# The projection stage of a retention layer as a table of slots, with every engine's order stated

## The chip, the cores and the metric

The kernel runs on one core of one Trainium2 chip. The core has five engines with an instruction stream each: PE (matrix multiply), DVE (vector), ACT (scalar functions), POOL (GpSimd) and SP, which here only issues DMAs. The metric is the time of one execution on the device in microseconds (us); lower is better.

## The reference, cut to what matters

One inference step of a two-layer decoder: 1024 prompt tokens and 8 decode tokens of width 1024 go through a retention layer (called layer 1 here) and then a sliding-window attention layer. The change is in the first part of layer 1:

```python
h = rmsnorm(x, g_norm)
proj = h @ w_in                                  # 1024 -> 6144
q, k, v, gate = jnp.split(proj, [RET_QK, 2 * RET_QK, 2 * RET_QK + RET_V], axis=-1)
...
S_new = S * gamma_h + k_t^T v_t                  # for the 8 decode tokens: state_ret in, new state out
o_t = q_t S_new                                  # 4 heads, each state is 256 x 512 floats
```

All is float32. The kernel splits each operand into a high part of reduced precision and the rest, and multiplies three times (high by high, high by rest, rest by high).

## The kernel before, in words

**The stage.** `_trunk` runs the stages one after the other. The first one, everything from the pool `sa` up to `sa.close()`, computes the projection for all tokens, and beside it updates the retention state of the 8 decode tokens. Its results go to scratch memory in DRAM (`qks`, `vsc`, `gsc`, `vscr`), from where the next stage reads them. The columns of `w_in` are worked off in 20 sets: q, k and v for each of 4 heads, then 8 sets for the gate.

**Opening.** The tokens come in as 8 chunks of 128 and one of 8 decode rows (`xload`, on SP's queue). Each is normalised (`xnorm`: a square with sum on ACT, a scale on DVE, a power on POOL, the scaling on DVE), transposed on PE (`xtrans`), and its halves and their sums and differences are split into high part (`XH`, ACT) and rest (`XL`, DVE or POOL) by `xeven`, `xodd` and `xthird`. The first two sets (q and k of head 0) are multiplied in the ordinary way as soon as the first chunks are there: 16 calls of `plain`, 24 matmuls each (line 471).

**Main part.** The 18 other sets run through `run_set`, each as 7 products instead of 8 (a Strassen-Winograd scheme), every product for two groups of tokens. A product is 12 matmuls for q, k and gate (lines 362 to 364) and 24 for v (355 to 357). The weights' quarters, or their sums (lines 199 to 209, POOL), are split before use by `prep_unit` (line 210 on ACT, 211 on DVE or POOL). After each product `after` takes the result out of its bank (ACT at lines 398 and 404, DVE at 400, 402, 406, 408 and 410), and `spill` writes it out with a DMA on SP's queue. Weights are loaded by DMAs on ACT's queue (`raw_load`).

**Decode.** Each of 64 steps (4 heads, 2 halves of the columns, 8 tokens) loads 256 KB of state into `st` (line 258) and a broadcast row into `vb` (260), both on SP's queue. It scales the state by gamma on ACT (267), adds `kd * vb` on DVE in two pieces (269), forms `yd = q S` on ACT (271) and DVE (272), splits `yd` into `yh` (276, ACT) and `yl` (277, POOL), writes the state back (273, SP) and adds `yh` and `yl` to a result bank with two matmuls (286, 287). `st` has 3 buffers and `yd` one. The generator `decode` emits, per step, the load of one step, the matmuls of the step four earlier and the state update of the step two earlier; `work` advances it once per 5.3 us of estimated PE time.

**What sets the order.** PE's order is written out by hand: `manual_schedule` is in force for PE alone. For DVE, ACT, POOL and SP the framework's own scheduler orders the emitted instructions by priority and its estimate of when they are ready. On the chip each of these engines then runs its instructions strictly in that order, each waiting for the semaphores that its data and buffers need.

Of the kernel before, what the change touches and what calls it, by code (L numbers as in the profile page):

```python
# [75 lines left out]
def _trunk(ctx, tc, nc, a):  # L76
# [21 lines left out]

    def tr(out, in_, ident, start=True, stop=True):
        nc.tensor.matmul(out, in_, ident, is_transpose=True, start=start, stop=stop)  # L100
# [18 lines left out]
    B11, B21, B22, T4, T1, T2, T3 = range(7)  # L119
    B11, B21, T3, B22, T2, T1, T4 = range(7)  # L120
    sa = ExitStack()
    dcp = sa.enter_context(tc.tile_pool(name="dcp", bufs=1, reuse_waits="tile"))
# [12 lines left out]
    nc.vector.memset(xdecr.bitcast(F32), 0.0)  # L135
    nc.vector.memset(xdecd.bitcast(F32), 0.0)
    onehot = dcp.tile([128, 64], F32, name="onehot")
# [3 lines left out]
    XT = {}  # L141

# [5 lines left out]
    XH, XL = [[[None] * 7, [None] * 7] for _ in range(2)]  # L148
    xalloc(0, xp0, 0, 7)
    xalloc(1, xp1, 0, 3)  # L150
# [6 lines left out]
    def ring():  # L157
        return evp.tile([128, 516], F32, tag="ev", bufs=10, name="ev")
# [8 lines left out]
    def raw_load(s):  # L167
        s.raw = []
        if s.kind == "v":
            for sub in range(2):  # L170
                for j in range(2):
                    t = raw_tile().rearrange("p (k f) -> p k f", k=2)
                    nc.scalar.dma_start(out=t, in_=w_in_ret[512 * j + 256 * sub:512 * j + 256 * sub + 256, s.c0:s.c0 + 512]
                                      .rearrange("(k p) f -> p k f", p=128))
                    s.raw.append(t)
        else:
            for j in range(2):
                t = raw_tile().rearrange("p (k f) -> p k f", k=4)
                nc.scalar.dma_start(out=t, in_=w_in_ret[512 * j:512 * j + 512, s.c0:s.c0 + 256]
                                  .rearrange("(k p) f -> p k f", p=128))  # L180
                s.raw.append(t)
# [5 lines left out]
    ORDER = ("A11", "S2", "S1", "A12", "S3", "S4", "A22")  # L187

    def prep_unit(s, name, sub):
        kk = 512 // s.fw  # L190
        sh = [128, kk, s.fw]

        t_ = [("s1", 2), ("s2", 2)] if (s.kind, s.h, name) == ("k", 0, "A22") else [("wop", 14)] * 2
        hi, lo = [wq.tile(sh, F32R, tag=t, bufs=n, name=nm) for (t, n), nm in zip(t_, ("woh", "wol"))]
        if name[0] == "A":
            src = quad(s, int(name[1]) - 1, int(name[2]) - 1, sub)
        elif name == "S2":
            s1 = s.s1[sub] = wq.tile(sh, F32, tag="s1", bufs=2, name="s1")
            nc.gpsimd.tensor_tensor(s1, quad(s, 1, 0, sub), quad(s, 1, 1, sub), ALU.add)
            src = s.s2[sub] = wq.tile(sh, F32, tag="s2", bufs=2, name="s2")  # L200
            nc.gpsimd.tensor_tensor(src, s1, quad(s, 0, 0, sub), ALU.subtract)
        elif name == "S1":
            src = s.s1.pop(sub)
        elif name == "S3":
            src = wq.tile(sh, F32, tag="s1", bufs=2, name="s3")
            nc.gpsimd.tensor_tensor(src, quad(s, 0, 0, sub), quad(s, 1, 0, sub), ALU.subtract)
        else:
            src = s.s2.pop(sub)
            nc.gpsimd.tensor_tensor(src, quad(s, 0, 1, sub), src, ALU.subtract)
        nc.scalar.activation(hi, src, AF.Copy)  # L210
        (nc.gpsimd if name in ("A12", "A22") else nc.vector).tensor_tensor(lo, src, hi.bitcast(F32), ALU.subtract)  # L211
        s.op[name, sub] = (hi, lo)

    def mkset(kind, h, c0, kt=0):
        s = Set()
        s.kind, s.h, s.c0, s.kt = kind, h, c0, kt
        s.fw = 256 if kind == "v" else 128
        s.subs = 2 if kind == "v" else 1
        s.op, s.s1, s.s2 = {}, {}, {}
        return s  # L220
# [10 lines left out]
    units = [(s, name, sub) for i, s in enumerate(sets) for name in (ORDER if i >= PLAIN else  # L231
             ("A11", "A12", "A21", "A22")) for sub in range(s.subs)]
    nprep = [0]
    nraw = [0]
    AHEAD = 5

    def raw_to(n):
        while nraw[0] < min(n, len(sets)):
            raw_load(sets[nraw[0]])
            nraw[0] += 1  # L240

    def prep_to(n):

        while nprep[0] < min(n, len(units)):
            i = sets.index(units[nprep[0]][0])
            raw_to(i + (1 if i < PLAIN else 2))
            prep_unit(*units[nprep[0]])
            nprep[0] += 1

# [5 lines left out]
    def dec_load(h, hf, b):  # L255
        d = heads[h]
        st = dpo[0].tile([128, 2, 256], F32, name="st", bufs=3)
        nc.sync.dma_start(out=st, in_=state_ret[0, b, h, :, hf * 256:hf * 256 + 256].rearrange("(f p) e -> p f e", p=128))
        vb = dpo[0].tile([128, 256], F32, name="vb", bufs=3)
        nc.sync.dma_start(out=vb, in_=vscr[h, b, hf * 256:hf * 256 + 256].partition_broadcast(128))  # L260
        d["d", hf, b] = (vb, st)

    def dec_state(h, hf, b):
        d = heads[h]
        qd, kd16 = d["qd"], d["kd"]
        vb, st = d.pop(("d", hf, b))
        nc.scalar.activation(st, st, AF.Copy, scale=GAM[h])  # L267
        for f in range(2):
            nc.vector.scalar_tensor_tensor(st[:, f, :], vb, kd16[:, f, b:b + 1], st[:, f, :], ALU.mult, ALU.add)  # L269
        yd = dpo[0].tile([128, 256], F32, name="yd")  # L270
        nc.scalar.activation(yd, st[:, 0, :], AF.Copy, scale=qd[:, 0, b:b + 1])
        nc.vector.scalar_tensor_tensor(yd, st[:, 1, :], qd[:, 1, b:b + 1], yd, ALU.mult, ALU.add)  # L272
        nc.sync.dma_start(out=nrs[0, b, h, :, hf * 256:hf * 256 + 256].rearrange("(f p) e -> p f e", p=128), in_=st)
        yh = dpo[0].tile([128, 256], F32R, name="yh", bufs=2)
        yl = dpo[0].tile([128, 256], F32R, name="yl", bufs=2)
        nc.scalar.activation(yh, yd, AF.Copy)  # L276
        nc.gpsimd.tensor_tensor(yl, yd, yh.bitcast(F32), ALU.subtract)  # L277
        d["y", hf, b] = (yh, yl)

    def dec_mm(h, hf, b):  # L280
        d = heads[h]
        if hf == 0 and b == 0:
            d["od"] = odp.tile([128, 512], F32, name="od")
        od = d["od"][0:8, hf * 256:hf * 256 + 256]
        yh, yl = d.pop(("y", hf, b))
        mm(od, oneh_r[:, b, :], yh, start=(b == 0), stop=False)
        mm(od, oneh_r[:, b, :], yl, start=False, stop=(b == ND - 1))

    def dec_norm(h):
        d = heads[h]  # L290
        od = d["od"][0:8, :]
        on = ring()[0:8, 0:512]
        ss = dcp.tile([128, 1], F32, name="oss", bufs=2)
        rs = dcp.tile([128, 1], F32, name="ors", bufs=2)
        nc.scalar.activation(on, od, AF.Square, accum_out=ss[:8])
        nc.vector.tensor_scalar(ss[:8], ss[:8], 1.0 / DV, EPS, ALU.mult, ALU.add)
        rsq(rs[:8], ss[:8], 1)
        nc.vector.tensor_scalar(on, od, rs[:8], None, ALU.mult)
        d["ond"] = on

    def dec_out(h):
        on = heads[h].pop("ond")
        pt = odp.tile([128, 512], F32, name="od")
        for i in range(4):
            tr(pt[:, i * 8:i * 8 + 8], on[:, i * 128:i * 128 + 128], ident[:8, :8])
        nc.vector.tensor_copy(odT[:, 4 * h:4 * h + 4, :], pt[:, :32].rearrange("p (i t) -> p i t", i=4))

    dsteps = []
    for h_ in range(H):
        dsteps += [(h_, hf, b) for hf in range(2) for b in range(ND)] + [None]  # L310

    def decode():

        for i in range(len(dsteps) + 4):
            ld, mm_, st = [dsteps[j] if 0 <= j < len(dsteps) else None for j in (i, i - 4, i - 2)]
            if ld:
                dec_load(*ld)
            if mm_:
                dec_mm(*mm_)
                if mm_[1:] == (1, ND - 1):  # L320
                    dec_norm(mm_[0])
            elif i >= 4:
                dec_out(dsteps[i - 5][0])
            if st:
                dec_state(*st)
            yield

    pend = []
    spent = [0.0]

    def work(us):

        if pend:
            spent[0] += us
            if spent[0] > 5.3:
                spent[0] -= 5.3
                next(pend[0], None)


# [38 lines left out]
    def run_set(s):  # L378
# [7 lines left out]
        def out_of(key, t):  # L386
            if s.kind == "v":
                c[key, t] = ring()[:, 0:n]
            elif t == 0:
                r = ring().rearrange("p (t n) -> p t n", t=2)  # L390
                c[key, 0], c[key, 1] = r[:, 0], r[:, 1]
# [1236 lines left out]
```

## Time and profile before

| | us |
|---|---|
| runs of the kernel | 1477.28, 1478.95, 1483.41 (median 1478.95) |
| the profiled execution | 1477.93 |
| its span, first to last instruction | 1476.1 |
| its mean granted TensorE clock | 0.968 |

In the profile a group of instructions is named by line, engine and operation, then output<-input. "Busy" is the time in which an engine executes. PE's matmuls overlap each other, so that PE can be 100% busy at half its rate: the number of matmuls in a stretch (x) tells the rate. "Idle before" is time in which an engine stood still ahead of an instruction, with what released it. The clock is the share of its full clock that TensorE was granted.

### The profile page before, as it was taken

How to read it: one execution, taken by the hardware profiler on the slowest of the kernel's cores; microseconds unless marked ns; L12 is line 12 of the kernel's file. 1: busy time of each engine (PE TensorE's matmuls, PEld its weight loads, DVE VectorE, ACT ScalarE, POOL GpSimd, SP SyncE). 2: the span in 40 equal slices, each digit the busy share in tenths (PEclk: the TensorE clock that was granted, in tenths of full speed). 3: DMA queues.
4: the chain of work that ended last, by engine and by line, in shares of the span. 5: the costliest groups of instructions: out<-in, count | busy, mean ns of one | idle time of the engine just before them, and what ended most of it. 6: DMA issues, size and time to landing. Idle time of an engine off the chain costs nothing.

```text
span 1476.1 us, 26259 instructions
## 1 busy us (share of the span) xinstructions
PE 1357.8 (92%) x9545; PEld 1277.5 (87%) x9545; DVE 835.0 (57%) x1783; ACT 665.4 (45%) x1698; POOL 727.6 (49%) x825
## 2 busy tenths in 40 slices
PE   6899987988998898989997999999999999997998
PEld 5899987988998798967776788998899989996998
DVE  5735546546565455447676211223689888989511
ACT  5533423433435454446765011224567666666411
POOL 4654525534554454448887655546456555444100
PEclk9999998998999999989999999999999999999999
DMA  5325645645556555265653534453211110103433
GB/s 176 114 86 169 190 126 165 187 134 181 174 169 181 172 166 161 61 191 165 202 162 126 182 116 149 118 161 114 76 40 44 38 44 26 55 16 97 141 88 83
DMA packets 192376, 186.18 MB, mean 126 GB/s; under 512 B 12549, under 2 KB 172093, under 8 KB 192230
## 3 DMA queue, kind: packets, MB, share of 16 engines
q1 hardware_dynamic: 152288, 143.62, 32.6%
q10 hardware_dynamic: 39958, 40.88, 8.7%
q8 instruction: 75, 1.23, 0.4%
q14 instruction: 55, 0.45, 0.1%
HBM read 128.09 MB, written 57.41 MB: 126 GB/s over the span
## 4 chain that ended last, share of the span: by engine, by line
PE 38%; DVE 16%; issue 10%; DMA 10%; ACT 8%; POOL 7%; ACTq 0%; DVEq 0%; SPq 0%; POOLq 0%
DMA st<-in_state_ret_dram 6%; PE pj L928 4%; PE pj L926 4%; PE pj L927 4%; PE pj L877 3%; PE pj L879 3%; PE pj L878 3%; PE b L362 2%; PE b L363 2%; PE b L364 2%; PE tr L100 2%; ACT s L1286 1%; DVE yd L272 1%; DVE Sl L785 1%; POOL yl L277 1%
## 5 line engine op out<-in xcount | busy, mean ns | idle before, releaser
L362 PE MATMUL b<-xh,woh 128*128 128x258 f32 x784 | 231.4, 295 | 31.2 <-DVE ev L406 20.0
L364 PE MATMUL b<-xh,wol 128*128 128x258 f32 x784 | 228.4, 291 | 0.0
L363 PE MATMUL b<-xl,woh 128*128 128x258 f32 x784 | 228.1, 291 | 0.0
L362 PEld LDWEIGHTS b<-xh,woh 128*128 128x128 f32 x784 | 155.3, 198 | 37.2 <-DVE ev L406 22.2
L877 PE MATMUL pj<-A_hi,wh 128*128 128x384 f32 (+1 forms) x512 | 173.0, 338 | 0.6 <-ACT Qd L1185 0.6
L879 PE MATMUL pj<-A_hi,wl 128*128 128x384 f32 (+1 forms) x512 | 165.5, 323 | 0.0
L878 PE MATMUL pj<-A_lo,wh 128*128 128x384 f32 (+1 forms) x512 | 165.4, 323 | 0.0
L363 PEld LDWEIGHTS b<-xl,woh 128*128 128x128 f32 x784 | 155.9, 199 | 0.0
L364 PEld LDWEIGHTS b<-xh,wol 128*128 128x128 f32 x784 | 155.1, 198 | 0.0
L269 DVE SCALAR_TENSOR_TENSOR st<-vb,kd,st 128x256 f32<-128x256 f32 x128 | 85.0, 683 | 122.4 <-ACT st L267 119.1
L867 POOL TENSOR_TENSOR wl<-wr,wh 128x512 fp32r<-128x512 f32 (+1 forms) x68 | 124.3, 1846 | 52.5 <-DVE wh L866 20.5
L355 PE MATMUL b<-woh,xh 128*128 128x256 f32 x448 | 129.8, 290 | 10.0 <-DVE ev L406 10.0
L356 PE MATMUL b<-wol,xh 128*128 128x256 f32 x448 | 129.3, 289 | 0.0
L357 PE MATMUL b<-woh,xl 128*128 128x256 f32 x448 | 129.2, 288 | 0.0
L267 ACT ACTIVATE st<-st 128x512 f32<-128x512 f32 x64 | 40.2, 630 | 158.6 <-DMA st<-in_state_ret_dram 125.6
L277 POOL TENSOR_TENSOR yl<-yd,yh 128x256 fp32r<-128x256 f32 x64 | 56.0, 876 | 111.4 <-ACT yh L276 100.8
L1291 POOL TENSOR_TENSOR s<-s,sm 128x512 f32<-128x512 f32 x64 | 68.0, 1063 | 69.3 <-ACT ot L1326 14.3
L877 PEld LDWEIGHTS pj<-A_hi,wh 128*128 128x128 f32 x512 | 97.8, 191 | 1.1 <-ACT Qd L1185 0.9
L878 PEld LDWEIGHTS pj<-A_lo,wh 128*128 128x128 f32 x512 | 97.9, 191 | 0.0
L355 PEld LDWEIGHTS b<-woh,xh 128*128 128x128 f32 x448 | 87.9, 196 | 11.3 <-DVE ev L406 10.8
L879 PEld LDWEIGHTS pj<-A_hi,wl 128*128 128x128 f32 x512 | 97.4, 190 | 0.0
L211 POOL TENSOR_TENSOR wol<-raw,woh 128x512 fp32r<-128x512 f32 x48 | 64.2, 1337 | 56.9 <-ACT woh L210 52.4
(352 smaller groups left out, 3971.6 us busy)
## 6 DMA issues: line engine op xcount, KB each, us to landing
raw<-in_w_in_ret_dram ACTq DMA_DIRECT2D x48, 512.0 KB
st<-in_state_ret_dram SPq DMA_DIRECT2D x64, 256.0 KB
out_dram<-st SPq DMA_DIRECT2D x64, 256.0 KB
wr<-in_w_out_ret_dram SPq DMA_DIRECT2D x32, 512.0 KB
wr<-in_w_in_swa_dram SPq DMA_DIRECT2D x18, 512.0 KB
qks<-ev SPq DMA_DIRECT2D x64, 128.0 KB
vsc<-ev SPq DMA_DIRECT2D x32, 256.0 KB
vb<-vscr SPq DMA_DIRECT2D x64, 128.0 KB
```

Of the source, the lines that this page charges most:

```text
L269: nc.vector.scalar_tensor_tensor(st[:, f, :], vb, kd16[:, f, b:b + 1], st[:, f, :], ALU.mult, ALU.add)
L277: nc.gpsimd.tensor_tensor(yl, yd, yh.bitcast(F32), ALU.subtract)
L355: mm(dst, xh, wh, start=a and i == 0, stop=False, skip_group_check=True)
L356: mm(dst, xh, wl, start=False, stop=False, skip_group_check=True)
L357: mm(dst, xl, wh, start=False, stop=z, skip_group_check=True)
L362: mm(dst, wh, xh, start=a, stop=False, **sg)
L363: mm(dst, wh, xl, start=False, stop=False, **sg)
L364: mm(dst, wl, xh, start=False, stop=z, **sg)
L867: lo_eng[0].tensor_tensor(lo[:, js, :], raw[:, i:i + step, :], hi.bitcast(F32)[:, js, :], ALU.subtract)
L877: mm(ps, hi[:, k, fs], xh[:, k, t0:t1], start=first and k == ks[0], stop=False)
L878: mm(ps, hi[:, k, fs], xl[:, k, t0:t1], start=False, stop=False)
L879: mm(ps, lo[:, k, fs], xh[:, k, t0:t1], start=False, stop=last and k == ks[-1])
```

## The change

The mathematics, the sets, the products and PE's matmuls per product stay. What changes:

- **All engines in a stated order.** Within the pool `sa` the manual schedule also holds for ACT, DVE, POOL and SP.
- **A table of slots.** Each `plain` and each product for one token group is a slot with an estimated PE time; the running sum of these is a clock. The evacuation of slot n is emitted in slot n+1, its spill in slot n+2 (n+3 where a SiLU comes between). Everything else has a planned time on that clock: a product's high split 6.5 us ahead of its first use (7.8 and 6.3 us for the two parts of v), the rest 1.4 us after it, weight loads up to 13 us ahead of their first use, and the decode steps every 5.3 us.
- **Decode rearranged.** The load of a step is planned 10.5 us ahead of its first arithmetic. ACT forms `kv = kd * vb` in two pieces (new tile, one buffer), and one DVE instruction over 128x512 does `st = gamma * st + kv`; the scale of the state on ACT is gone. `yd` comes 13.9 and 15.3 us after the load, `yh` 16.8, `yl` 18.2, the matmuls are placed at the first slot boundary after 20.4 us. `st` gets 4 buffers instead of 3, `yd` 2 instead of 1, `yl` 1 instead of 2.
- **Opening rearranged.** The gain row is broadcast by one DMA instead of two matmuls with a row of ones. The raw weights of the first two sets are loaded on SP's queue between the chunks. The chunks are normalised in place; the transposed copies of the even chunks are taken by DVE (ACT before); the scale ahead of the power is on POOL (DVE before). The 16 plain slots each carry a written list of chunk work, and transposes of chunks 1, 3, 4, 6, 5, 7 open the slots 2, 3, 6, 7, 9, 10. The decode rows' columns are split piece by piece on DVE.
- **Buffers.** The ring of 10 evacuation buffers becomes four rings (3, 2, 2, 2); split weights have 12 buffers instead of 14; `qd`/`kd` 4 instead of 2.

```diff
+    sa.enter_context(tc.manual_schedule(engines={ET.Activation, ET.DVE, ET.Pool, ET.SP}))
...
-    def dec_load(h, hf, b):
-        d = heads[h]
-        st = dpo[0].tile([128, 2, 256], F32, name="st", bufs=3)
+    def dec_load(d, h, hf, b):
+        d["st"] = dt("st", 4, (128, 2, 256))
+        nc.sync.dma_start(out=d["st"], in_=sview(state_ret, h, hf, b))
+        d["vb"] = dt("vb", 3)
+        nc.sync.dma_start(out=d["vb"], in_=vscr[h, b, hf * 256:hf * 256 + 256].partition_broadcast(128))
...
-        nc.scalar.activation(st, st, AF.Copy, scale=GAM[h])
-        for f in range(2):
-            nc.vector.scalar_tensor_tensor(st[:, f, :], vb, kd16[:, f, b:b + 1], st[:, f, :], ALU.mult, ALU.add)
+    def dec_kv(d, h, hf, b):
+        d["kv"] = dt("kv", 1, (128, 2, 256))
+        for f in range(2):
+            act(d["kv"][:, f, :], d["vb"], AF.Copy, scale=heads[h]["kd"][:, f, b:b + 1])
+
+    def dec_st(d, h, hf, b):
+        dve.scalar_tensor_tensor(d["st"], d["st"], GAM[h], d["kv"], MUL, ADD)
+
+    def dec_y0(d, h, hf, b):
+        d["yd"] = dt("yd", 2)
+        act(d["yd"], d["st"][:, 0, :], AF.Copy, scale=heads[h]["qd"][:, 0, b:b + 1])
+        nc.sync.dma_start(out=sview(nrs, h, hf, b), in_=d["st"])
...
+    def slot(us, pe, *ops):
+        s = Slot()
+        s.t, s.pe, s.ops = clock[0], pe, ops
+        clock[0] += us
+        slots.append(s)
+        return len(slots) - 1
+
+    def later(n, fn, *a):
+
+        at.setdefault(n, []).append((fn, a))
+
+    def when(t, fn, *a):
+        ev.append((t, len(ev), fn, a))
...
+        us = 2.84 if s.kind == "v" else 1.43
+        slot((us + (0.95 if dec else 0.0)) * (1.045 if s is not sets[2] else 1.0), pe)
+        later(n + 1, evac, s, j, t)
...
+    STEP, GAP = 5.3, 6.5
+    pes = []
+    t0 = 0.0
+    for h in range(H):
+        t0 = max(t0 + GAP, sets[3 * h + 2].end + 10.0)
+        for hf in range(2):
+            for b in range(ND):
+                d = {}
+                for dt_, fn in ((0.0, dec_load), (10.5, dec_kv), (12.3, dec_st), (13.9, dec_y0), (15.3, dec_y1),
+                                (16.8, dec_yh), (18.2, dec_yl)):
+                    when(t0 + dt_, fn, d, h, hf, b)
+                pes.append((t0 + 20.4, dec_mm, (d, h, hf, b)))
+                m = t0 + 20.4
+                t0 += STEP
...
+    nc.scalar.dma_start(out=gb, in_=norm_ret[0].partition_broadcast(128))
+    nc.scalar.dma_start(out=ident, in_=a["c1"][:, 0:128])
+    act(warm, warm, AF.Silu)
+    for c in (8, 0, 2):
+        xload(c)
+    for r in range(2):
+        raw_load(q0, r, nc.sync)
+    for c in (1, 3):
+        xload(c)
+    for r in range(2):
+        raw_load(k0, r, nc.sync)
+    for c in (4, 6, 7):
+        xload(c)
...
+    for n, s in enumerate(slots):
+        while pes and pes[0][0] <= s.t:
+            _, fn, args = pes.pop(0)
+            fn(*args)
+        s.pe()
+        for fn, args in at.pop(n, ()):
+            fn(*args)
+        for fn, args in s.ops:
+            fn(*args)
+        end = s.t if n + 1 == len(slots) else slots[n + 1].t
+        while ev and ev[0][0] < end:
+            _, _, fn, args = ev.pop(0)
+            fn(*args)
```

More of the change, by code (lines that the diff above doesn't have):

```diff
@@ L688, in _trunk @@
+    rest = sorted([(t, 0, fn, args) for t, _, fn, args in ev] + [(t, 1, fn, args) for t, fn, args in pes],
+                  key=lambda e: e[:2])
+    for _, _, fn, args in rest:
+        fn(*args)
+    print("stage", clock[0], "decode", t0)
     sa.close()
```

751 lines of the change are left out of this document (376 added, 375 removed).

## The prediction

> **What bounds the kernel now.** I read the page first, then the busy time by stretches, then who waits for whom in the projection stage, then the chain that ended last inside one slow stretch.
>
> ```profile
> span 1476.1 us, 26259 instructions
> ...
> PE 1357.8 (92%) x9545; PEld 1277.5 (87%) x9545; DVE 835.0 (57%) x1783; ACT 665.4 (45%) x1698; POOL 727.6 (49%) x825
> ```
>
> PE looks full, but overlapping matmuls count as busy, so the rate has to be read from the counts. The next rows are stretches: length, PE, PEld, DVE, ACT and POOL busy (with counts), granted clock, DMA share, GB/s. The last one was asked for PE alone.
>
> ```profile
> 87.00:638.00 551.00, 502.08 (x3952) 490.55 (x3950) 297.05 (x495) 221.47 (x474) 257.77 (x310) 0.95 0.52 156
> 280.00:320.00 40.00, 40.00 (x340) 39.60 (x339) 18.73 (x28) 14.31 (x29) 16.18 (x19) 1.00 0.47 140
> 200.00:240.00 40.00, 31.05 (x210) 29.37 (x209) 18.57 (x26) 12.45 (x26) 13.86 (x12) 0.84 0.52 161
> 420.00:440.00 20.00, 20.00 (x171) 19.76 (x170) 13.04 (x19) 9.06 (x18) 10.67 (x10) 1.00 0.79 243
> 520.00:540.00 20.00, 20.00 (x165) 19.77 (x165) 13.78 (x23) 10.77 (x25) 11.06 (x15) 0.98 0.58 171
> ...
> 140.00:160.00 20.00, 17.56 (x144) 1.00 0.69 191
> ```
>
> From 280 to 320 us PE runs 340 matmuls in 40 us, 0.1176 us each at a clock of 1.00: the full rate. The main part of the stage, 87 to 638 us, holds 3952 of them. At the full rate that is 464.9 us; it takes 551. So 86.1 us are lost there, and that is what this stage could give back. The stretch from 200 to 240 shows how: 210 matmuls need 24.7 us, PE is idle 8.95, and the other 6.35 go to a clock of 0.84.
>
> The waits in the stage (in total, times, longest):
>
> ```profile
> ACT st L267 <- DMA st<-in_state_ret_dram: 125.6, 39, 6.4
> DVE st L269 <- ACT st L267: 119.1, 42, 6.4
> ...
> PE b L362 <- DVE ev L406: 20.0, 8, 4.2
> PE b L362 <- DVE ev L410: 10.7, 8, 2.4
> PE b L355 <- DVE ev L406: 10.0, 4, 3.7
> ```
>
> ACT stands before the state's scale until the state has landed, DVE stands before line 269 for ACT, and PE waits for banks that DVE has not emptied. The chain inside the slow stretch (start, length) says why the load comes late:
>
> ```profile
> 212.77 6.83 DMA st<-in_state_ret_dram
> ...
> 219.71 0.64 ACT st L267
> ...
> 220.77 0.68 DVE ev L406
> ...
> 222.83 1.51 DVE yd L272
> ...
> 224.36 2.70 DMA st<-in_state_ret_dram
> ```
>
> A load starts when a `yd` ends, since its buffer comes free then; it takes 2.7 to 6.8 us; the next `yd` on ACT is queued behind the scale that waits for this load. With 3 buffers, only one load is in flight at a time: 11.6 us from one load to the next here, where PE's order wants a step each 5.3 us.
>
> **The change part by part: the main part.** The decode chain's order is undone at its root. The load is now planned 12.3 us ahead of the one instruction that needs it, against 6.8 us for the longest load above, with four buffers instead of three. The wait does not vanish, it moves: DVE now waits for the state itself. Queued behind it are DVE's evacuations and weight splits, and PE waits for those. A lead of 12.3 against 6.8 is the cover; without it each microsecond of lateness would stop DVE. ACT's new wait is for `vb`, 10.5 us after its issue. SP's load waits for the write-back of the step four earlier, issued 7.3 us before it; the spills stand behind that.
>
> Durations for the parts (busy, mean ns):
>
> ```profile
> L269 DVE SCALAR_TENSOR_TENSOR st<-vb,kd,st 128x256 f32<-128x256 f32 x128 | 85.0, 683 | 122.4 <-ACT st L267 119.1 <-ACT woh L210 1.7 <-DMA vb<-vscr 1.2
> L211 DVE TENSOR_TENSOR wol<-s,woh 128x512 fp32r<-128x512 f32 x88 | 74.3, 846 | 27.4 <-ACT woh L210 23.8 <-PE b L471 2.7 <-issue 0.2
> L211 POOL TENSOR_TENSOR wol<-raw,woh 128x512 fp32r<-128x512 f32 x48 | 64.2, 1337 | 56.9 <-ACT woh L210 52.4 <-PE b L364 2.4 <-PE b L357 1.9
> L277 POOL TENSOR_TENSOR yl<-yd,yh 128x256 fp32r<-128x256 f32 x64 | 56.0, 876 | 111.4 <-ACT yh L276 100.8 <-DVE st L269 5.4 <-PE b L357 4.7
> L267 ACT ACTIVATE st<-st 128x512 f32<-128x512 f32 x64 | 40.2, 630 | 158.6 <-DMA st<-in_state_ret_dram 125.6 <-issue 18.9 <-DVE ev L408 6.1
> L271 ACT ACTIVATE yd<-st,qd 128x256 f32<-128x256 f32 x64 | 32.6, 509 | 64.4 <-POOL yl L277 62.7 <-DVE st L269 1.6
> L533 DVE TENSOR_TENSOR xl<-b,xh 128x512 fp32r<-128x512 f32 x16 | 10.4, 685 | 7.2 <-ACT xh L532 7.2
> L513 DVE SCALAR_TENSOR_TENSOR raw<-xq,rs,gb 128x1024 f32<-128x1024 f32 x7 | 10.0, 1428 | 6.7 <-POOL rs L114 6.7
> L533 DVE TENSOR_TENSOR xl<-ev,xh 128x512 fp32r<-128x512 f32 x8 | 9.5, 1203 | 0.0
> L511 DVE TENSOR_SCALAR ss<-ss 128x1 f32<-128x1 f32 x8 | 1.0, 145 | 2.1 <-ACT raw L510 2.1
> ```
>
> Decode work: ACT loses 64 scales (40.2 us) and gains 128 pieces of 128x256, nearest line 271, so 128 x 0.509 = 65.2: plus 25. DVE loses 128 pieces (85.0) and gains 64 of 128x512; on the line between 0.683 for 256 columns and 1.428 for 1024 that is 0.93 each, 60 us: minus 25 (bounds: 54 us by line 211's 0.846, 87 by twice 0.683). None of it is on the path as long as the engines keep up: squeezed into some 480 us, DVE would be busy (297.05 - 25)/480 = 57%, ACT (221.47 + 25)/480 = 51%, POOL 257.77/480 = 54%. From 520 to 540 us they were at 69, 54 and 55% while PE ran 165 matmuls of 170 possible. The DMAs, 551 x 156 = 86 MB, would need 179 GB/s; from 420 to 440 us they ran at 243 with PE at its full 171.
>
> What is late next is the end of the decode chain. `yl` is planned at 18.2 and takes 0.876, so it ends at 19.1, and the matmuls stand at 20.4: a margin of 1.3 us. In front of the chain can lie one weight split on DVE (0.846) and one on POOL (1.337), 2.2 us together. The worst is then 0.9 us of PE waiting in each of 64 steps, 58 us; the best is nothing. The matmuls are put at the first slot boundary after their time, which with slots of 12 x 0.1176 = 1.41 us adds 0.7 on average. I take 0.2 us per step, nearer to the lower end: 13 us. A bank has at least three slots, 4.2 us, between its evacuation's start and PE's next use, as much as the longest wait that the table of waits shows, and those came from the 6.4 us holds that go. So the evacuations get no price. Main part: 86.1 - 13 = **73 us gained** (bounds 28 and 86).
>
> Does a short wait cost more than itself? From 140 to 160 us PE was idle 2.44 us in pieces and the clock stayed at 1.00; from 200 to 240, with longer ones, each idle microsecond cost 15.3/8.95 = 1.7. I price short waits at themselves. The Trainium skill, "TensorE: Matmul & The Clock Gate", section "A second HAM failure mode: psum-queue depth-cycling", speaks against that: frequent tiny idles between groups of matmuls can be enough to make the clock swing. By that rule the 13 us would cost 13 x 1.7 = 22 and the sum would be 9 us higher; the row from 140 to 160 us does not bear it out.
>
> **The opening.**
>
> ```profile
> 9.92 1.28 DVE L513 SCALAR_TENSOR_TENSOR raw<-xq,rs,gb 128x1024 f32<-128x1024 f32 x1 [0.67 <-POOL rs L114]
> ...
> 13.63 1.28 DVE L513 SCALAR_TENSOR_TENSOR raw<-xq,rs,gb 128x1024 f32<-128x1024 f32 x1
> ```
> ```profile
> 14.97 1.97 PE L100 MATMUL b<-ident,raw 128*128 128x128 f32 x8 [1.74 <-DVE raw L513]
> 19.30 2.09 PE L471 MATMUL b<-xh,woh 128*128 128x258 f32 x8 [2.36 <-ACT xh L532]
> 21.19 1.77 PE L471 MATMUL b<-xh,wol 128*128 128x258 f32 x8
> 22.80 1.12 PE L471 MATMUL b<-xl,woh 128*128 128x258 f32 x8
> ...
> 84.93 0.28 PE L355 MATMUL b<-woh,xh 128*128 128x256 f32 x1
> ```
> ```profile
> 16.15 0.63 ACT L210 ACTIVATE woh<-raw 128x512 fp32r<-128x512 f32 x1 [2.68 <-DMA raw<-in_w_in_ret_dram]
> ```
> ```profile
> 5.00:10.00 5.00, 2.24 (x9) 1.00 1.04 401
> ```
>
> The first projection matmul is at 19.30 us. Chunk 2 was scaled at 13.63, behind a weight split that waited; in the stated order it follows chunk 0, at 9.92 + 1.28 + 0.2 = 11.4. Its transposes then end at 11.4 + 1.3 + 2.0 = 14.7, and a high split of 0.6 lets PE start at 15.3. The raw weights, which landed at 16.15, come ahead of chunks 1 to 6 in SP's queue. The broadcast of the gain moves another 0.5 MB while the DMAs are full (share 1.04, 401 GB/s): 1.3 us, which can eat some of it. **4 us gained** (bounds 0 and 6).
>
> From 19.30 to 84.93, 65.6 us, run 16 x 24 matmuls and 6 x 8 transposes: 432 x 0.1176 = 50.8 us. The first 16 took 3.5 us (19.30 to 22.80) instead of 1.9, a start that stays: 52.4. What is left, 13.2 us, was waiting. In the slots 5 to 11 of the list DVE gets 16 operations from a bank (0.685), 7 from SBUF (1.203), 2 scalings (1.428) and 18 small ones (0.145): 11.0 + 8.4 + 2.9 + 2.6 = 24.9 us, against 7 x 24 + 4 x 8 = 200 matmuls, 23.5 us. DVE is thus a little short there. I leave 4 us of waiting: **9 us gained** (bounds 0 and 13).
>
> The other edits have one answer, nothing: fewer ring and weight buffers are reused more than a set later or 11 us after their product, and the copies that go from ACT to DVE are counted in the slots above.
>
> **The sum.** 4 + 9 + 73 = 86 us off the profiled execution's 1477.93: 1391.9. That execution took 1.8 us beyond its span, and is 1.0 under the median of the runs, 1478.95; so **1393 us** for a median.
>
> **The rivals.** *The decode chain becomes PE's wait at its worst.* Every step is 0.9 us late, 58 us instead of 13: 1393 + 45 = 1438. For it: margins of 1.3 us behind queues whose single operations take as long. Against it: the slot boundaries, and that a PE that waits hands all others time.
>
> *The hold moves to DVE and grows (slower).* SP's load waits for a write-back, the DMAs carry 15% more per microsecond, and a late state now stops the engine that empties the banks. It ends slower when the stage's waits exceed 86.1 + 13.2 + 7.4 = 107 us, 1.7 us in each step; as DVE has 12.3 us of lead, loads would have to take some 14 us on average. At 2 us a step, 128 instead of 13, it gives 1393 + 115 = 1508. Against it: the longest load seen is 6.8 us.
>
> *The clock swings on short waits*, the skill's rule above: 1402.
>
> *The change does not do what it says*: some resource that I do not see paces the decode steps as before, the 73 us stay, and only the opening gains or loses: about 1477, no change. The stretches with PE at full rate inside the decode stage speak against it.
>
> **How the numbers follow.** My case has 0.68, the clock rival 0.05, the late chain 0.18: all faster, 0.91. No change has 0.03, the hold on DVE 0.06. The lower end takes all bounds at their best, 6 + 13 + 86 = 105 off: 1374. The upper end is the late chain, 1438. About 0.5%, 7.4 us, is what a measurement can tell from no change.
>
> **What would show it.** Right: the first projection matmul near 15 us, the first v matmul near 72, the last gate evacuation near 552; ACT's wait for the state gone, and DVE's wait for it under some 10 us in total; state loads at an even 5.3 us; long stretches at 170 matmuls per 20 us with the clock at 1.00; PE's remaining waits mostly on `yl`. Wrong: DVE idle on the state load or SP on the write-back for microseconds at a time, a clock under 0.95 in the stage, or PE waiting for weight splits. The stages behind should keep their length; if they don't, the sum is wrong in a term that I left out.

## The result, and the profile after

| | before | after |
|---|---|---|
| median (range, runs), us | 1479.56 (1477.28 to 1483.41, 4) | 1387.83 (1386.91 to 1390.77, 4) |
| profiled execution, us | 1477.93 | 1390.77 |
| its span, us | 1476.1 | 1389.0 |

The ratio of after to before is 0.938, with a 95% interval of 0.936 to 0.941: 91.7 us less in the medians, 87.1 us less between the two profiled spans. The profiled execution of after is the slowest of its four runs, 2.9 us above the median.

The page of the kernel after begins so, and its chain that ended last is made up so (shares by engine):

```profile
span 1389.0 us, 26326 instructions
...
PE 1320.1 (95%) x9541; PEld 1249.1 (90%) x9541; DVE 804.3 (58%) x1737; ACT 679.3 (49%) x1754; POOL 739.5 (53%) x830
...
PE 65%; DVE 15%; ACT 6%; issue 6%; POOL 4%; DMA 3%; ACTq 0%; DVEq 0%; POOLq 0%; SPq 0%
```

The same line of the page of before:

```profile
PE 38%; DVE 16%; issue 10%; DMA 10%; ACT 8%; POOL 7%; ACTq 0%; DVEq 0%; SPq 0%; POOLq 0%
```

PE's share of the chain went from 38 to 65%, and the DMAs' from 10 to 3%. The boundaries of the stage in the timeline of after (start, length): first projection matmul, first v matmul, last evacuation of a gate product.

```profile
14.09 0.74 PE L555 MATMUL b<-xh,woh 128*128 128x258 f32 x4
...
70.82 0.28 PE L332 MATMUL b<-woh,xh 128*128 128x256 f32 x1
...
546.54 0.43 DVE L380 TENSOR_TENSOR evp<-b,evp 128x258 f32<-128x258 f32 x1 [0.97 <-PE b L341]
```

In before, the first two stand in the prediction (19.30 and 84.93), and the third is:

```profile
638.18 0.43 DVE L410 TENSOR_TENSOR ev<-b,ev 128x258 f32<-128x258 f32 x1 [0.97 <-PE b L364]
```

So the 87.1 us are 5.2 ahead of the first projection matmul, 8.9 in the opening (65.6 to 56.7), 77.5 in the main part (553.2 to 475.7), and -4.5 in the stages behind (837.9 to 842.5).

Busy time by stretches in after (length, PE, PEld, DVE, ACT, POOL, clock, DMA share, GB/s; the last was asked for PE alone):

```profile
71.00:546.00 475.00, 473.77 (x3966) 468.92 (x3966) 261.79 (x438) 240.02 (x542) 267.66 (x312) 1.00 0.60 182
220.00:240.00 20.00, 20.00 (x168) 19.66 (x167) 10.32 (x22) 10.35 (x24) 13.06 (x16) 1.00 0.82 258
...
80.00:540.00 460.00, 460.00 (x3853) 1.00 0.62 187
```

The whole main part comes close to the density that before had in its good stretches, 3966 matmuls in 475 us for 340 in 40, and the clock stays at 1.00. What PE waited for in the stage, the five longest (in total, times, longest):

```profile
PE tr L840 <- DMA qk<-qks: 7.3, 2, 5.4
PE pd L105 <- DMA ident<-const_c_dram: 7.2, 1, 7.2
PE b L105 <- DVE xq L441: 2.3, 2, 2.1
PE b L555 <- POOL wol L223: 1.5, 1, 1.5
PE b L333 <- DVE wol L223: 1.2, 1, 1.2
```

The first belongs to the next stage, the next three to the start and the opening. Of the main part only the last row is left, 1.2 us: PE waits neither for a bank nor for `yl`. The waits of the others that touch the decode step:

```profile
ACT yd L269 <- DVE st L265: 42.6, 25, 3.1
POOL yl L281 <- PE od L288: 41.6, 18, 5.1
...
DVE st L265 <- ACT kv L262: 7.2, 8, 1.5
```

The two waits of over 100 us each for the state (ACT's for the load, DVE's for ACT) are gone, and no such wait of DVE for the load stands in their place. The waits left are long only in sum, and POOL's is for PE: the chain runs ahead of PE and not behind it.

### The profile page after: what moved, and what is told of

Read it like the earlier page. It is cut to its first block, busy times and chain, and to the rows that moved or that the text cites. A ratio compares the mean times of both kernels' runs of the same rounds, so it can differ in the third digit from the quotient of the medians.

```text
span 1389.0 us, 26326 instructions
## 1 busy us (share of the span) xinstructions
PE 1320.1 (95%) x9541; PEld 1249.1 (90%) x9541; DVE 804.3 (58%) x1737; ACT 679.3 (49%) x1754; POOL 739.5 (53%) x830
## 4 chain that ended last, share of the span: by engine, by line
PE 65%; DVE 15%; ACT 6%; issue 6%; POOL 4%; DMA 3%; ACTq 0%; DVEq 0%; POOLq 0%; SPq 0%
PE b L339 7%; PE b L341 7%; PE b L340 7%; PE b L333 4%; PE b L334 4%; PE b L332 4%; PE pj L1037 4%; PE pj L1035 4%; PE pj L1036 4%; PE pj L986 3%; PE pj L987 3%; PE pj L988 3%; ACT s L1395 2%; PE tr L105 2%; DVE Sl L894 1%
## 5 line engine op out<-in xcount | busy, mean ns | idle before, releaser
L339 PE MATMUL b<-xh,woh 128*128 128x258 f32 x784 | 222.1, 283 | 0.0
L341 PE MATMUL b<-xh,wol 128*128 128x258 f32 x784 | 221.7, 283 | 0.0
L340 PE MATMUL b<-xl,woh 128*128 128x258 f32 x784 | 221.3, 282 | 0.0
L339 PEld LDWEIGHTS b<-xh,woh 128*128 128x128 f32 x784 | 148.1, 189 | 1.2
L340 PEld LDWEIGHTS b<-xl,woh 128*128 128x128 f32 x784 | 148.6, 190 | 0.0
L341 PEld LDWEIGHTS b<-xh,wol 128*128 128x128 f32 x784 | 148.0, 189 | 0.0
L332 PE MATMUL b<-woh,xh 128*128 128x256 f32 x448 | 125.7, 281 | 0.0
L223 POOL TENSOR_TENSOR wol<-raw,woh 128x512 fp32r<-128x512 f32 x52 | 68.8, 1330 | 47.9 <-ACT woh L218 47.0
L333 PEld LDWEIGHTS b<-wol,xh 128*128 128x128 f32 x448 | 84.3, 188 | 1.4 <-DVE wol L223 1.4
L1395 ACT ACTIVATE s<-s,mx 128x256 f32<-128x256 f32 x128 | 64.0, 502 | 43.9 <-DVE mx L1392 39.6
```

The lines of the kernel that those rows point to most:

```text
L223: eng.tensor_tensor(lo, src_of(s, name, sub), hi.bitcast(F32), SUB)
L332: mm(dst, xh, wh, start=a and i == 0, stop=False, skip_group_check=True)
L333: mm(dst, xh, wl, start=False, stop=False, skip_group_check=True)
L339: mm(dst, wh, xh, start=a, stop=False, **sg)
L340: mm(dst, wh, xl, start=False, stop=False, **sg)
L341: mm(dst, wl, xh, start=False, stop=z, **sg)
```

## The experiments

In all of them the whole reference is computed. Two numbers come back throughout. The **main part** is the time from the first v matmul to the last gate evacuation, as above (before 553.2 us, after 475.7). The **lead** is the time from the issue of a state's load on SP to the start of the first instruction that uses the state (ACT's scale in before, DVE's line 265 in after); given is the median over the 64 steps: before 3.7 us, after 14.1. One pair of each, first the load's issue and then the use, in after:

```profile
215.44 0.46 SPq L255 DMA_DIRECT2D st<-in_state_ret_dram  x1
...
228.74 0.70 DVE L265 SCALAR_TENSOR_TENSOR st<-st,kv 128x512 f32<-128x512 f32 x1
```

and in before:

```profile
231.82 0.37 SPq L258 DMA_DIRECT2D st<-in_state_ret_dram  x1
...
234.75 0.63 ACT L267 ACTIVATE st<-st 128x512 f32<-128x512 f32 x1 [4.79 <-DMA st<-in_state_ret_dram]
```

13.3 us against 2.9, the latter with ACT standing still for 4.79 us ahead of the use.

My theory at first was that the buffers and the arithmetic, which take the load out of ACT's way, carry most of the gain, with the order only keeping the loads ahead. (The prediction itself counted on the lead, and didn't say which part of the change makes it.) The rival was that the stated order carries it. The first four kernels tell them apart.

**The framework's order for all engines but PE**, all else as after:

```diff
-    sa.enter_context(tc.manual_schedule(engines={ET.Activation, ET.DVE, ET.Pool, ET.SP}))
```

> The changed kernel without the one line that puts ACT, DVE, POOL and SP under the stated order; the program, its buffers and its decode arithmetic stay. My theory (the loop in the decode chain cost the time; fewer dependences and more buffers open it, the stated order keeps the loads ahead): 1410 us, DVE's wait for the state between 20 and 80 us in the stage. Rival 'order alone': 1450 to 1478. Rival 'decode data flow alone': 1386 to 1395, no wait of PE in the main part.

Measured: 1463.17 us (1459.33 to 1465.52), ratio to before 0.987 [0.985, 0.989]. Main part 545.0, lead 4.1. Waits and a stretch of it:

```profile
DVE st L264 <- DMA st<-in_state_ret_dram: 103.6, 39, 6.4
ACT kv L261 <- DVE st L264: 89.0, 36, 6.7
...
PE od L287 <- POOL yl L280: 34.0, 10, 7.5
...
PE b L338 <- DVE evw L375: 9.0, 4, 4.9
```
```profile
80.00:540.00 460.00, 411.11 (x3278) 0.95 0.59 173
```

This kernel has the four buffers, the new arithmetic and the table's order of emission, and yet the wait is back on another engine: DVE now stands before the state for 103.6 us, and ACT behind DVE, since `kv` has one buffer. How this reaches PE can be followed in the timeline:

```profile
172.53 0.69 DVE L264 SCALAR_TENSOR_TENSOR st<-st,kv 128x512 f32<-128x512 f32 x1 [4.86 <-DMA st<-in_state_ret_dram]
173.25 0.51 ACT L261 ACTIVATE kv<-vb,kd 128x256 f32<-128x256 f32 x1 [3.39 <-DVE st L264]
...
174.84 1.27 POOL L222 TENSOR_TENSOR wol<-raw,woh 128x512 fp32r<-128x512 f32 x1 [6.03 <-ACT woh L217]
...
176.06 0.72 POOL L280 TENSOR_TENSOR yl<-yd,yh 128x256 fp32r<-128x256 f32 x1
...
176.84 0.38 PE L287 MATMUL od<-yl,oneh_r 128*8 128x256 f32 x1 [5.06 <-POOL yl L280]
```

DVE stands for the load, ACT's next `kv` for DVE, the high split behind it in ACT's queue comes late, POOL stands for that split, `yl` is next in POOL's queue, and PE waits 5.06 us for `yl`. So most of PE's waits come through `yl` (34.0 us) and fewer through the evacuations, though the load is at the root. Nearly all of the main part's gain went with the stated order, 69.3 of 77.5 us, and 3.9 of the opening's 8.9. The theory falls.

**Before with after's decode buffers only:**

```diff
-        st = dpo[0].tile([128, 2, 256], F32, name="st", bufs=3)
+        st = dpo[0].tile([128, 2, 256], F32, name="st", bufs=4)
...
-        yd = dpo[0].tile([128, 256], F32, name="yd")
+        yd = dpo[0].tile([128, 256], F32, name="yd", bufs=2)
...
-        yl = dpo[0].tile([128, 256], F32R, name="yl", bufs=2)
+        yl = dpo[0].tile([128, 256], F32R, name="yl")
```

(The ring of evacuation buffers has 9 instead of 10, to make room.)

> The kernel before with 4 state buffers instead of 3 and 2 of yd instead of 1 (paid for by one yl buffer and one evacuation buffer less), nothing else. My theory: two loads can be in flight, ACT's wait for the state falls from 125.6 us to about 60 and the time to about 1435. Rival 'order alone': 1470 to 1480. Rival 'decode data flow alone': about 1470, since the scale on ACT still waits for the load.

Measured: 1470.46 us (1470.34 to 1471.44), ratio 0.992 [0.991, 0.994]. Main part 545.9, lead 4.3. ACT's wait has not become shorter but longer than the 125.6 us of before:

```profile
ACT st L267 <- DMA st<-in_state_ret_dram: 155.0, 45, 6.9
...
SPq L258 <- DVE yd L272: 56.6, 25, 7.6
```

The second row is SP's: the load still waits there for a `yd` to end and free a buffer. The timelines show where the fourth buffer went. In before, 62 of the 64 loads are issued with two earlier steps still short of their `yd`; here 61 are issued with three. But in 55 of 64 steps (52 in before) the scales of all earlier steps have begun by then. So the order uses the new buffer to scale one more state ahead of its `yd`, and the load is not issued earlier relative to its own use. What the buffers alone are worth isn't quite shown, since they are paid for: with one `yl` PE's waits for it rise from 0.8 to 20.2 us.

**Before with after's arithmetic** (`st` keeps 3 buffers; `yd` 2, `yl` 1, the ring 9):

```diff
-        nc.scalar.activation(st, st, AF.Copy, scale=GAM[h])
+        kv = dpo[0].tile([128, 2, 256], F32, name="kv")
         for f in range(2):
-            nc.vector.scalar_tensor_tensor(st[:, f, :], vb, kd16[:, f, b:b + 1], st[:, f, :], ALU.mult, ALU.add)
+            nc.scalar.activation(kv[:, f, :], vb, AF.Copy, scale=kd16[:, f, b:b + 1])
+        nc.vector.scalar_tensor_tensor(st, st, GAM[h], kv, ALU.mult, ALU.add)
```

> The kernel before with the new decode arithmetic (kv on ACT, one DVE instruction on the state) and 2 yd buffers (one yl and one evacuation buffer less), 3 state buffers, order by the framework. My theory: ACT no longer stands behind a load, yd comes earlier, 1425. Rival 'order alone': 1470 to 1480. Rival 'decode data flow alone': 1400 to 1410 (all but the opening).

Measured: 1494.98 us (1494.12 to 1495.56), ratio 1.009 [1.007, 1.010]: slower than before. Main part 568.5, lead 3.8.

```profile
DVE st L270 <- DMA st<-in_state_ret_dram: 118.7, 42, 6.6
...
PE od L288 <- POOL yl L278: 44.6, 14, 6.2
```

The hold did move to DVE, as the prediction's slower rival had it, and the main part is 15.3 us longer. PE's longest waits are for `yl`, along the same path as in the framework's order above: a held DVE stops ACT's `kv` too, and POOL's splits behind that. Whether a second `kv` buffer or a second `yl` would avoid it was not tried.

**After with the old arithmetic**, in the stated order:

```diff
-        d["kv"] = dt("kv", 1, (128, 2, 256))
-        for f in range(2):
-            act(d["kv"][:, f, :], d["vb"], AF.Copy, scale=heads[h]["kd"][:, f, b:b + 1])
+        act(d["st"], d["st"], AF.Copy, scale=GAM[h])
...
-        dve.scalar_tensor_tensor(d["st"], d["st"], GAM[h], d["kv"], MUL, ADD)
+        for f in range(2):
+            dve.scalar_tensor_tensor(d["st"][:, f, :], d["vb"], heads[h]["kd"][:, f, b:b + 1], d["st"][:, f, :], MUL, ADD)
```

> The changed kernel with the old decode arithmetic in the new places: at 10.5 us ACT scales the state, at 12.3 us DVE adds kd*vb in two pieces. My theory and 'order alone': the load has 10.5 us of lead against 6.8 us for the longest load seen, so 1386 to 1395. Rival 'decode data flow alone': ACT stands behind loads again, 1430 or more.

Measured: 1389.80 us (1388.70 to 1391.37), ratio 0.9375 [0.9355, 0.9395], not to be told from after. Main part 475.7, lead 11.0. So ACT can scale the state first without harm, when it comes to it 11 us behind the load. The arithmetic is worth nothing in the stated order, and less than nothing in the framework's.

Now the theory is: the stated order carries the gain, because it keeps the use of a state far behind its load. The next two ask which queue matters, SP's, which issues the loads, or the three that use them.

**SP's order alone stated:**

```diff
-    sa.enter_context(tc.manual_schedule(engines={ET.Activation, ET.DVE, ET.Pool, ET.SP}))
+    sa.enter_context(tc.manual_schedule(engines={ET.SP}))
```

> The changed kernel with the stated order for SP alone (the queue of the state loads, write-backs and spills); ACT, DVE and POOL go back to the framework's order. Theory 'the loads': late loads cost the time, because SP's queue held them behind things that came late; then 1395 to 1410. Theory 'the consumers': DVE and ACT are told to use a state right behind its load and stand there, whatever SP does; then 1440 to 1465, with DVE waiting for the state for some 100 us as with no order at all.

Measured: 1419.69 us (1419.24 to 1420.49), ratio 0.956 [0.953, 0.959]. Main part 499.9, lead 6.2. What is left of the waits:

```profile
ACT kv L262 <- DMA vb<-vscr: 77.2, 40, 5.2
...
PE od L288 <- POOL yl L281: 13.4, 6, 6.2
```

The time lies between the two ranges that were expected, so neither theory has it alone.

**ACT's, DVE's and POOL's order stated, SP's not:**

```diff
-    sa.enter_context(tc.manual_schedule(engines={ET.Activation, ET.DVE, ET.Pool, ET.SP}))
+    sa.enter_context(tc.manual_schedule(engines={ET.Activation, ET.DVE, ET.Pool}))
```

> The changed kernel with the stated order for ACT, DVE and POOL, and SP's queue in the framework's order. Theory 'the consumers': 1390 to 1400, PE without waits in the main part. Theory 'the loads': 1430 or more, DVE waiting for loads that SP issues late.

Measured: 1395.42 us (1391.53 to 1396.76), ratio 0.939 [0.936, 0.942]. Main part 484.4, lead 16.4. PE still waits a little for the chain's end:

```profile
PE od L288 <- POOL yl L281: 4.1, 3, 1.9
```

Of the 69.3 us of main part between the framework's order and the stated one, SP's alone gives 45.1 and the other three 60.6. They add up to more than the whole: either puts distance between load and use, and one is nearly enough. But the two also order everything else, evacuations and splits among it. The next kernel changes the distance by itself.

**After with the loads 8 us later:**

```diff
-                for dt_, fn in ((0.0, dec_load), (10.5, dec_kv), (12.3, dec_st), (13.9, dec_y0), (15.3, dec_y1),
+                for dt_, fn in ((8.0, dec_load), (10.5, dec_kv), (12.3, dec_st), (13.9, dec_y0), (15.3, dec_y1),
```

> The changed kernel with each decode load planned 8 us later: 4.3 us of lead to the DVE instruction on the state, 2.5 us to kv on ACT, all else in its place. Theory 'lead': loads of 2.7 to 6.8 us now come late in most steps, DVE waits about 1 to 2 us a step, which PE partly feels: 1400 to 1440. Rival 'order alone': once the order is stated, the lead does not matter: 1386 to 1392.

Measured: 1398.45 us (1397.42 to 1400.08), ratio 0.942 [0.939, 0.945]. Main part 484.9, lead 7.4.

```profile
ACT kv L262 <- DMA vb<-vscr: 79.5, 34, 6.7
...
PE od L287 <- ACT yh L277: 3.4, 2, 2.4
PE od L288 <- POOL yl L281: 3.2, 5, 1.0
```
```profile
80.00:540.00 460.00, 453.30 (x3776) 1.00 0.62 186
```

ACT now stands 79.5 us before `vb`, as long as in the kernel with SP's order alone, but this costs the main part only 9.2 us. DVE has no wait for the state itself: it is the broadcast row, loaded right behind the state and planned only 2.5 us ahead of `kv`, that comes late. So the lead matters, at 9 us for 7 us less of it; the time is between the two ranges that were expected. What the step from 7.4 down to 4.1 costs, where the lead comes under the longest load of 6.8 us, this kernel doesn't say.

**After with the matmuls of a step 2.1 us earlier**, which takes the margin behind `yl`:

```diff
-                pes.append((t0 + 20.4, dec_mm, (d, h, hf, b)))
+                pes.append((t0 + 18.3, dec_mm, (d, h, hf, b)))
```

> The changed kernel with the two matmuls of each decode step planned at 18.3 us instead of 20.4, that is, at the first slot boundary after yl is started instead of 1.3 us after its end. By my prediction's term (margin 1.3 us, queues of up to 2.2 us) PE now waits for yl in most steps, 0.5 us each, and the time is 1388 + 30 = 1418. Rival: the chain runs ahead of its plan, since POOL was seen waiting for PE and PE never for yl; then 1386 to 1392.

Measured: 1399.50 us (1398.56 to 1400.06), ratio 0.942 [0.939, 0.946]. Main part 486.1, lead 14.7.

```profile
PE od L288 <- POOL yl L281: 7.5, 9, 2.3
```
```profile
80.00:540.00 460.00, 451.64 (x3766) 1.00 0.62 186
```

The chain's end does become PE's wait when the margin is gone, in 9 of 64 steps, and the main part grows by 10.4 us, 0.16 per step. By my term (0.5 us in most steps, 30 us in all) it should have been more.

**After with before's buffers:**

```diff
-        d["st"] = dt("st", 4, (128, 2, 256))
+        d["st"] = dt("st", 3, (128, 2, 256))
...
-        d["yd"] = dt("yd", 2)
+        d["yd"] = dt("yd", 1)
```

> The changed kernel with 3 state buffers instead of 4 and 1 of yd instead of 2, as before the change; the stated order stays. A state buffer then has three steps, 15.9 us, from one load's issue to the next, while its life from load to yd is planned at 15.3 to 16 and the write-back has to land too. Theory 'the order carries it, the lead follows from it': SP issues loads some 3 to 5 us later than planned, the median lead from load to use falls from 14.1 to about 9 us, which still covers the loads: 1388 to 1398. Theory 'buffers': the loop closes again, 1430 or more.

Measured: 1394.62 us (1393.23 to 1400.09), ratio 0.942 [0.939, 0.944]. The profiled execution is its slowest: main part 488.4, lead 9.6.

```profile
SPq L255 <- DMA out_dram<-st: 174.3, 55, 8.1
```
```profile
PE od L288 <- POOL yl L281: 7.6, 6, 2.5
```

With three buffers the load waits on SP for the write-back of the step three earlier, 174.3 us in all, and the lead shrinks. In the medians that is 6.8 us; the intervals of the two ratios overlap a little (0.939 to 0.944, after 0.936 to 0.941), but PE's waits for `yl` in the trace are new. So the fourth buffer and the second `yd` seem to be worth a few microseconds once the order leaves room for them.

**The even chunks' copies back on ACT**, an edit of the opening, where DVE was the busiest beside PE:

```diff
-        dve.tensor_copy(half(c, j), PO[c][j])
+        act(half(c, j), PO[c][j], AF.Copy)
```

> The changed kernel with the transposed copies of the even chunks taken by ACT instead of DVE (8 copies of 128x512). In the opening of the changed kernel DVE is busy 47.8 us of 51, ACT 26.9. If DVE bounds the opening, the stretch from the first projection matmul to the first v matmul falls from 56.7 us by up to 4 (PE's idle time there) and the time by 2 to 4 us. If chunks or weights bound it, nothing changes (within 1 us).

Measured: 1386.06 us (1384.97 to 1388.74), ratio 0.936 [0.933, 0.938]. The two opening stretches, from the kernel after and from this one:

```profile
20.00:71.00 51.00, 48.20 (x398) 47.33 (x396) 47.82 (x74) 26.91 (x56) 39.06 (x48) 1.00 0.29 89
```
```profile
20.00:71.00 51.00, 48.90 (x404) 48.09 (x403) 46.06 (x70) 29.77 (x63) 42.17 (x49) 1.00 0.29 88
```

DVE loses 1.8 us of work and PE gets 6 more matmuls into the stretch; the opening takes 55.2 us instead of 56.7. DVE at 47.8 of 51 us was thus part of what is left there, but a small one. The interval of this kernel overlaps that of after.

**The same, with the start rearranged** (the identity's DMA first, the gain row's behind the first activation, chunk 0 ahead of the decode rows):

```diff
-    nc.scalar.dma_start(out=gb, in_=norm_ret[0].partition_broadcast(128))
     nc.scalar.dma_start(out=ident, in_=a["c1"][:, 0:128])
     act(warm, warm, AF.Silu)
-    for c in (8, 0, 2):
+    nc.scalar.dma_start(out=gb, in_=norm_ret[0].partition_broadcast(128))
+    for c in (0, 8, 2):
         xload(c)
```

> As the run with the copies on ACT, and chunk 0 is loaded first, the identity ahead of the gain row, which is issued some 2 us later. If the start waits for chunk 0's bytes among the others, the first projection matmul comes 1 to 1.5 us earlier than 14.1 and the time is 3 to 5 us under the changed kernel's; if not, as the run before.

Measured: 1386.27 us (1384.84 to 1387.34), ratio 0.935 [0.933, 0.938]. The first projection matmul is at 14.42 us, not earlier than after's 14.09, so the order of these three transfers isn't what holds the start. This kernel and the one above are the best of the study, by 1.6 to 1.8 us in the medians; the overlapping intervals don't tell them from after.

The stretches of eleven of the kernels in one table (us; all from the same three boundaries in the timeline of each):

| | start | opening | main | behind | lead |
|---|---|---|---|---|---|
| before | 19.3 | 65.6 | 553.2 | 837.9 | 3.7 |
| before, buffers | 19.2 | 65.5 | 545.9 | 838.2 | 4.3 |
| before, arithmetic | 19.1 | 64.9 | 568.5 | 841.1 | 3.8 |
| after, framework's order | 16.3 | 60.6 | 545.0 | 841.8 | 4.1 |
| after, SP's order alone | 16.6 | 60.6 | 499.9 | 840.4 | 6.2 |
| after, all but SP's | 14.2 | 56.8 | 484.4 | 839.6 | 16.4 |
| after, old arithmetic | 14.4 | 56.8 | 475.7 | 842.7 | 11.0 |
| after, late loads | 14.1 | 56.8 | 484.9 | 839.8 | 7.4 |
| after, no margin | 14.1 | 56.8 | 486.1 | 839.8 | 14.7 |
| after, before's buffers | 14.0 | 56.8 | 488.4 | 839.1 | 9.6 |
| after | 14.1 | 56.7 | 475.7 | 842.5 | 14.1 |

## Why the prediction was right, and where it was wrong

**The start and the opening** came out as worked out: 5.2 us gained for 4, 8.9 for 9. Of the opening's 8.9, 5.0 come without the stated order (65.6 to 60.6) and 3.9 with it.

**The main part's size** was nearly right, 77.5 for 73, but two of its terms were off and partly cancelled, which is luck. *The full rate.* The prediction took 0.1176 us per matmul from a stretch of 40 us, and 464.9 us for the whole. The starts of single matmuls in the timeline of after say more:

```profile
73.05 0.28 PE L332 MATMUL b<-woh,xh 128*128 128x256 f32 x1
...
75.18 0.28 PE L332 MATMUL b<-woh,xh 128*128 128x256 f32 x1
...
539.83 0.28 PE L339 MATMUL b<-xh,woh 128*128 128x258 f32 x1
...
545.98 0.28 PE L339 MATMUL b<-xh,woh 128*128 128x258 f32 x1
```

18 matmuls of 256 columns lie between the first two, 2.13/18 = 0.118 us each, and 51 of 258 columns between the last two, 6.15/51 = 0.1206 each. The rate was read in a stretch where 310 of the 338 matmuls that start have 256 columns, while 2352 of the 3968 of the main part have 258; and the count of a stretch also holds the matmuls that straddle its edges, 340 for 338. Both made the rate look better. Without its last 1.2 us of waiting the main part is 474.5 us, against 553.2 - 86.1 = 467.1 by the prediction: the floor was taken 7.4 us too low. *The late chain.* It was priced at 13 us, 0.2 for each of 64 steps; it measured nothing, since the only wait left is the 1.2 us above. 13 - 1.2 - 7.4 = 4.4 is what the gain came out larger by (77.5 - 73, but for rounding). The margin that the table leaves is enough: only taking away 2.1 us of it brought 10.4 us, 0.16 per step, near what I had put on the change itself.

**The cause** was half right. The prediction rested the main part's gain on a load planned 12.3 us ahead of its use, and the runs bear that out: the lead is 14.1 us and the two long waits are gone. What failed is the step that laid the loss to the buffers, "With 3 buffers, only one load is in flight at a time", and counted the fourth buffer into the cover without asking which part of the change makes the lead. Decode buffers put into before bring 0.8%, the arithmetic costs 0.9%, and after without the stated order keeps 1.3% of its 6.2%. What the runs show in its place: in the framework's order the use of a state is placed right behind its load (lead 3.7 to 4.3 us, with 3 or 4 buffers), each engine runs strictly in that order, and so ACT or DVE stands, with work that PE needs queued behind it. In the stated order the use comes 14 us behind the load and the wait disappears; with the old arithmetic it comes 11 us behind and the main part is the same.

The lead may not be all. Leads of 6.2 and 7.4 us gave main parts of 499.9 and 484.9, with waits of ACT for `vb` of 77.2 and 79.5 us. The first of these kernels leaves ACT, DVE and POOL in the framework's order, so the order of the splits and evacuations around the decode steps can be worth up to 15 us by itself; that is argued from two kernels whose leads are close, not shown. Open too is why the framework puts the use so close behind the load: the traces show only the order that came out. The program of before with all engines in the order in which it emits was not tried.

**The clock.** The prediction priced short waits at themselves, against the rule that it drew from the Trainium skill, "TensorE: Matmul & The Clock Gate", section "A second HAM failure mode: psum-queue depth-cycling", that frequent tiny idles can make the clock swing. In after there are too few of them to tell. With the late loads and without the margin PE idled 460 - 453.30 = 6.7 and 460 - 451.64 = 8.4 us between 80 and 540 us, in pieces of 2.4 us and less. The granted clock in those rows is 1.00, but that is a mean over 460 us. The 20 us around the longest wait read otherwise, with the late loads (2.4 us) and with before's buffers (2.5 us):

```profile
420.00:440.00 20.00, 17.10 (x132) 0.91 0.60 187
```
```profile
300.00:320.00 20.00, 17.52 (x136) 0.91 0.78 240
```

A clock of 0.91 is 1.8 us of the 20 on top of 2.9 and 2.5 us of idle time, so these waits cost 1.6 to 1.7 times themselves, about as the longer ones of before did. Length alone doesn't decide: without the margin, with pieces of up to 2.3 us, no stretch of 20 us in the main part shows such a fall, while with all but SP's order stated the clock is 0.91 from 460 to 480 us, around a wait of 1.9 us. So the price of a short wait at itself was too low for some of them, and the rule is borne out in part: what the clock followed here were single waits of about 2 us, and that many tiny ones do the same isn't shown. The clock is 0.95 with the framework's order, where PE waits up to 7.5 us at a time.

**The rivals.** The hold that moves to DVE and makes the kernel slower is real, but it needs the framework's order: it is what the arithmetic alone did (1494.98 us). The late chain needs a margin 2.1 us smaller to appear. The rest that the prediction named as signs came so: 14.09 for 15 us, 70.82 for 72, 546.54 for 552, clock 1.00, 168 matmuls per 20 us for 170. Two did not. PE's remaining waits are not on `yl`. And the loads are not at an even 5.3 us: the 64 of after begin with the first of these rows and end with the second, 5.74 us apart on average, with about half of the gaps over 5.5 and one in ten over 8.4.

```profile
117.77 1.32 SPq L255 DMA_DIRECT2D st<-in_state_ret_dram  x1
...
479.10 0.43 SPq L255 DMA_DIRECT2D st<-in_state_ret_dram  x1
```

**Durations.** The groups of the new instructions (busy, mean ns):

```profile
L265 DVE SCALAR_TENSOR_TENSOR st<-st,kv 128x512 f32<-128x512 f32 x64 | 53.9, 843 | 7.4 <-ACT kv L262 7.2
L262 ACT ACTIVATE kv<-vb,kd 128x256 f32<-128x256 f32 x128 | 57.5, 498 | 3.1 <-DMA vb<-vscr 2.1 <-ACT yd L269 0.6 <-ACT evc L374 0.4
```

0.843 us for 0.93, at the lower bound that was given, and 0.498 for 0.509. Neither lies on the path: replacing both by the old instructions changed nothing.

**The stages behind** were put at no change and are 4.5 us longer in the profiled execution, as much as the main part gained beyond its 73 us. That the spans fell by 87.1 us where the sum has 86 is thus in part luck. All kernels share the code there, and their values run from 837.9 to 842.7 us without a pattern in what was edited; the kernel with DVE spared in the opening has 838.9. The cause is open. The spread is also the limit of what differences of a few microseconds between spans can say here.

## What to carry to other kernels

Where an engine runs its queue strictly in order, look at the distance from a load's issue to its first use. If it is no longer than the load itself, look first at the order: here a fourth buffer alone left the distance as it was, and ordering the use later removed the wait. A chain of small steps beside a busy PE is best given both a lead ahead of its first use and a margin behind its last step; here each was worth about 10 us. When a change brings an order, buffers and new arithmetic at once, forecast each by itself: the total can come out right for a cause that is half wrong.

## What the runs showed of the hardware

At a clock of 1.00, matmuls of 258 columns followed each other every 0.1206 us and those of 256 columns every 0.118, in the rows above. Over the whole main part of after, neighbours of the same shape are 0.1203 and 0.1184 us apart: 1.6% more time for 0.8% more columns. The granted clock fell behind single waits of PE of 1.9, 2.4 and 2.5 us (0.91 over the 20 us around each), and not behind one of 2.3 us. And the DMAs did not hinder PE at 258 GB/s, with 168 matmuls in 20 us.
